# Attention probabilities of a hybrid decoder: two complementary triangles transposed as one tile and parted by 0/1 masks, transposes issued ahead of the value products

## The chip, the core and the metric

The kernel runs on one core of a Trainium2 chip. Its engines are TensorE (PE, matrix products; the profile shows its weight loads as PEld), VectorE (DVE), ScalarE (ACT), GpSimd (POOL, unused here) and SyncE (SP, which issues the DMAs). The metric is device time in microseconds for one call, the median of some runs.

## The reference

Two decoder layers on 256 tokens of width 2048, all in float32. Layer 0 is a recurrent block (RG-LRU) with a SwiGLU FFN, layer 1 a grouped-query attention with a sliding window and attention sinks, with a second FFN. The part that matters here:

```
scores = einsum("bnqhgd,bnkhd->bnhgqk", q, k_band) * (1.0 / sqrt(HEAD_DIM))
mask = window_mask(nblk)            # 0 <= q_pos - k_pos < 128, and the key exists
scores = where(mask, scores, -1e30)
probs = softmax(concatenate([scores, sink], -1), -1)[..., :-1]
out = einsum("bnhgqk,bnkhd->bnqhgd", probs, v_band)
x = x + out.reshape(b, s, N_HEADS * HEAD_DIM) @ w_o
```

There are 32 query heads of 64 features, four K/V heads, and two blocks of 128 tokens. A query of block 0 sees only the keys of its own block that are not after it (a lower triangle). A query of block 1 sees the same triangle of its own block, and of block 0 the keys k > q (in positions inside the block): the complementary triangle.

## The kernel before, in words

Activations are held transposed, features on the partitions and the 256 tokens along the row. Every weight matrix is streamed from HBM as jobs: one job is a tile of 128x1024 (512 KB), loaded by SP four jobs ahead, split three jobs ahead into a high part (ACT, line 259) and a rest (DVE, line 260), and multiplied in 24 matmuls of 256 columns (products, lines 289 to 325; some pairs are merged into one of 512 columns). A group is the run of jobs that fills four PSUM banks: 8 jobs for the q projection w_q (four groups) and for w_o. The first two groups of w_o are interleaved (project, lines 492 to 505): six jobs of the first, six of the second, then the last two of each. Each job of w_o multiplies two of the sixteen attention tiles at[0] to at[15].

All else is background: generators in a list, in order of their start, which stream (line 271) advances twice per job, once in the middle (half_tick) and once at the end (run_bg). A job so has two ticks. run_bg (line 200) keeps an account for DVE and one for ACT. Every helper charges a cost in ns (lines 111 to 137: ACT 100 + 0.833 a column, a DVE tensor_tensor 69 + 1.042 a column, a tensor_scalar 69 + 0.6 a column), at each tick DVE_TICK and ACT_TICK are taken off, but not below -SPARE, and steps run while both accounts are under their tick. In the attention stage these are 740, 900 and 1000 (LATER, line 810). pe (line 115) takes the estimated time of TensorE's extra work off both accounts. A step that yields n rests for n ticks. If a job needs a tile that isn't ready, need (line 213) steps all background tasks, whatever the accounts say, until it is. The program's scheduler may move instructions of one engine past each other where no dependence forbids it; pe_other (line 327) chains the extra TensorE instructions in the order in which they are written.

The attention (attn, line 850) has, for each group of w_q, a q task (line 987): it squares and splits the four q tiles, holds one PSUM bank for three ticks (matmuls with con, a copy, two transposes), and then puts four pairs of heads into todo. One generator, pairs (line 926), works them off, one visit at a time and 19 visits in all (V1 to V19 in what follows). A visit has three parts, each for another pair of heads: values of pair A (values, line 861), transposes of pair B (line 873), scores of a new pair (line 881). Thus the pair that is new in visit n is transposed in visit n+2 and multiplied with the values in visit n+3. After the matmuls, a tick later, the transposes are copied from PSUM by ACT (lines 958 and 959), the value product is split into its two parts (ACT, DVE), which makes at[k] ready, and softmax (line 892) runs for the new pair: per head and query block a masked scaling with its maximum on DVE (line 900), exponentials with sums on ACT, and then four multiplications by the reciprocal of the sum on DVE (lines 918 to 922, through ts, line 131).

A visit needs up to four PSUM banks of the four that MISC allows, so it waits while a q task holds one. It also waits while hold is set, which is from the seventh job of a group to the start of the next group. The next visit comes VISIT = 3 ticks after the last began, or when its softmax is done.

The probabilities of one head are a tile of 128 queries x 384: columns 0 to 127 for block 0 on its own keys, 128 to 255 for block 1 on the keys of block 0, 256 to 383 for block 1 on its own keys. Masked scores become exact zeros. All three parts are transposed, six transposes for two heads.

Of the kernel before, what the change touches and what calls it, by code (L numbers as in the profile page):

```python
# [15 lines left out]
ALU = mybir.AluOpType  # L16

P = 128
D = 2048
T = 256  # L20
# [14 lines left out]

K_ONE, K_BLK, K_SEL0, K_SEL1, K_ID = 0, 128, 256, 384, 512
K_HS, K_MASK = 640, 672
NCON = 672 + 384


class Val:
# [7 lines left out]
class Trunk:  # L49
# [18 lines left out]
    def __init__(self, ctx, tc, dram):  # L68
# [6 lines left out]
        self.par = const.tile([P, NPAR], F32, name="par")  # L75
        self.con = const.tile([P, NCON], F32, name="con")
        self.cc = const.tile([P, 32], F32, name="cc")
# [772 lines left out]
    def attn(self, xs, r, gains, rn):  # L850
        nc, con, par = self.nc, self.con, self.par
# [5 lines left out]
        blocks = ((0, 0, P), (1, P, 3 * P))  # L857
# [3 lines left out]
        def values(k, pT, p):  # L861

            c = (k // 4) * HD
            v0, v1 = (q.ap[:, c:c + HD] for q in self.v)
            o = [p[HD * hh:HD * hh + HD, T:2 * T] for hh in range(2)]
            for hh in range(2):
                self.pe_other(o[hh], v0, pT[0][:, hh * T:(hh + 1) * T], start=True, stop=False)
            for hh in range(2):
                self.pe_other(o[hh][:, P:T], v1, pT[1][:, hh * P:(hh + 1) * P], start=False, stop=True)
            for q in pT:  # L870
                self.free(q)

        def transposes(sc, ps):
            for hh in (1, 0):
                for j in (2, 1, 0):
                    o = ps[0][:, hh * T + j * P:hh * T + j * P + P] if j < 2 else ps[1][:, hh * P:hh * P + P]
                    self.pe_other(o, sc[hh][:, j * P:(j + 1) * P], one, f=nc.tensor.transpose)
            for q in sc:
                self.free(q)

        def scores(k, qs, ps):

            kd = self.kd[k // 4].ap
            for b, c0, c1 in blocks:
                for i, j in ((1, 0), (0, 0), (0, 1)):
                    for hh in range(2):
                        q = slice(HD * hh, HD * hh + HD)
                        self.pe_other(ps[hh][:, c0:c1], qs[q, i * T + b * P:i * T + b * P + P],
                                      kd[q, j * T:j * T + c1 - c0], start=i == 1, stop=j == 1)
            self.free(qs)  # L890

        def softmax(k, rr, ps, sc):
            f = k % 4
            sm = self.half()
            mx, nm, es, den = (sm[:, 4 * i:4 * i + 4] for i in range(4))
            for hh in range(2):
                for b, c0, c1 in blocks:
                    i = b * 2 + hh
                    self.dve += 69 + 1.042 * (c1 - c0)
                    nc.vector.tensor_tensor_reduce(  # L900
                        sc[hh][:, c0:c1], ps[hh][:, c0:c1], con[:, K_MASK + c0:K_MASK + c1],
                        rr[:, b * 8 + f * 2 + hh:b * 8 + f * 2 + hh + 1],
                        par[:, C_SINK + 4 * k + hh:C_SINK + 4 * k + hh + 1], ALU.add, ALU.max,
                        accum_out=mx[:, i:i + 1])
                self.free_mbank(ps[hh])
                yield
            self.ts(nm, mx, -1.0, None, ALU.mult)
            self.tt(es, par[:, C_SINK + 4 * k:C_SINK + 4 * k + 4], mx, ALU.subtract)
            self.a(es, es, AF.Exp)
            for hh in range(2):  # L910
                for b, c0, c1 in blocks:
                    i = b * 2 + hh
                    o = sc[hh][:, c0:c1]
                    self.a(o, o, AF.Exp, bias=nm[:, i:i + 1], accum_out=den[:, i:i + 1])
                yield
            self.tt(den, den, es, ALU.add)
            self.rcp(den, den)
            for hh in range(2):
                for b, c0, c1 in blocks:
                    i = b * 2 + hh  # L920
                    o = sc[hh][:, c0:c1]
                    self.ts(o, o, den[:, i:i + 1], None, ALU.mult)
                yield
            self.free_half(sm)

        def pairs():


            A = B = C = None
            n = 0  # L930
            while n < ND or A or B or C:
                new = None
                if todo and self.kd[todo[0][0] // 4].ready and self.v[0].ready and self.v[1].ready:
                    new = todo.popleft()
                    n += 1
                elif not (A or B or C):
                    yield 1
                    continue
                at_tick = self.tick
                count = 2 * bool(A or B) + 2 * bool(new)  # L940
                while self.hold or self.misc + count > self.MISC or len(self.banks) < count or len(self.slots) < 6:
                    yield 1
                pt = [self.mbank() for _ in range(2)] if A or B else None
                ps = [self.mbank() for _ in range(2)] if new else None
                if A:
                    values(A[0], A[1], pt[1])
                    self.pe(900)
                if B:
                    transposes(B[1], pt)
                    self.pe(700)  # L950
                if new:
                    scores(new[0], new[1], ps)
                    self.pe(900)
                yield 1
                nextA = None
                if B:
                    s = [self.slot(F32) for _ in range(2)]
                    self.a(s[0], pt[0])
                    self.a(s[1][:, 0:T], pt[1][:, 0:T])
                    nextA = (B[0], s)  # L960
                    yield
                if A:
                    s = self.slot()
                    self.split_act(s, pt[1][:, T:2 * T])
                    at[A[0]].ap = s
                    at[A[0]].ready = True
                    yield
                for p in pt or ():
                    self.free_mbank(p)
                A, B, C = nextA, C, None  # L970
                if new:
                    sc = [self.slot(F32) for _ in range(2)]
                    yield from softmax(new[0], new[2], ps, sc)
                    C = (new[0], sc)
                yield max(1, at_tick + self.VISIT - self.tick)
            for q in self.kvs:
                self.free(q)

        for g in range(4):
            def done(ps, g=g):  # L980
# [6 lines left out]
                def task():  # L987
# [41 lines left out]
                    if g == 0:  # L1029
                        self.spawn(pairs())  # L1030
# [50 lines left out]
def constants():  # L1081
    i = np.arange(P)
    con = np.zeros((P, NCON), np.float32)
    con[:, K_ONE:K_ONE + P] = 1.0
    con[:, K_BLK:K_BLK + P] = (i[:, None] // HD) == (i[None, :] // HD)
    con[:, K_SEL0:K_SEL0 + P] = i[:, None] == (i[None, :] % HD)
    con[:, K_SEL1:K_SEL1 + P] = i[:, None] == (HD + i[None, :] % HD)
    con[:, K_ID:K_ID + P] = np.eye(P)
    con[:, K_HS:K_HS + 32] = (i[:, None] // HD) == np.arange(32)[None, :] // 16
    own = np.where(i[None, :] <= i[:, None], 0.0, NEG)  # L1090
    prev = np.where(i[None, :] > i[:, None], 0.0, NEG)
    con[:, K_MASK:K_MASK + 384] = np.concatenate([own, prev, own], axis=1)
    return con


# [35 lines left out]
```

## Time and profile before

| | |
|---|---|
| median of 3 runs | 1989.83 us (1989.81 to 1989.93) |
| span of the profiled execution | 1988.6 us; the page gives no time of that execution outside the span |
| scores of the first visit | at 1072.85 us of the span |
| values of the last visit | at 1208.33 us |
| matmuls that are not of a weight stream, L334 | 1.6% of the chain that ended last |
| granted TensorE clock | full in all 40 slices |

Times inside the trace are us from the start of the span. A row of the timeline gives start, length, engine, line, operation, out<-in by the program's names (buffer numbers left out), shape and count; a bracket at its end is idle time of the engine before it, and what ended it. For a matmul the shape 128*64 128x256 is a stationary operand of 128 rows and 64 columns, and 256 columns streamed. b is any PSUM bank, s any slot of SBUF, con the table of constants. So b<-con,s is a transpose of probabilities, b<-s,s with 128*64 is a value product and with 64*128 a score, b<-s,hi and b<-s,lo are the weight streams, and b<-s,con and b<-con,h belong to a q task. The first instruction of such a chain may stand under line 331 and the others under 334. A row of a group has busy time, mean ns of one, and idle time before. In a row of windows stand the window, its length, and the busy time and count of PE, PEld, DVE, ACT, POOL, the clock, the DMA share and GB/s.

### The profile page before, as it was taken

Reading aid. Unit: us, or ns where it says so; the run is one execution under the profiler, and the core shown is the slowest. Engines: PE = TensorE matmul, PEld = TensorE weight load, DVE = VectorE, ACT = ScalarE, POOL = GpSimd, SP = SyncE. Lnnn points to the kernel's source line nnn. Section 1 sums busy time; section 2 is a strip of 40 time slices with the busy share of each in tenths; the row PEclk is TensorE's granted clock in tenths of the full one; section 3 lists DMA queues with packets and bytes.
Section 4 is the critical chain, followed back from the end, with each engine's and each line's share of the span. In section 5 each row is a group of like instructions: output and inputs, shape, how many; then the busy total and the mean of one; then the engine's idle time right before and its main releaser. Section 6 shows DMA issues by size and latency. Waiting matters only on the chain.

```text
span 1988.6 us, 40066 instructions
## 1 busy us (share of the span) xinstructions
PE 1982.0 (100%) x16684; PEld 1935.5 (97%) x16684; DVE 1271.2 (64%) x2049; ACT 1067.9 (54%) x1624; POOL 0.2 (0%) x4
## 2 busy tenths in 40 slices
PE   9999999999999999999999999999999999999999
PEld 9999999999999999999999889999999999999999
DVE  8988876556556655545668786755565565554453
ACT  7798655444444444444556775544454454444442
POOL 0000000000000000000000000000000000000000
PEclk9999999999999999999999999999999999999999
DMA  8555655565556555556555435565566656656663
GB/s 279 185 187 182 211 191 192 196 196 191 192 195 196 191 192 196 195 191 194 197 186 167 134 101 163 188 197 195 191 193 196 195 191 194 197 193 203 204 208 128
DMA packets 105302, 376.58 MB, mean 189 GB/s; under 512 B 11808, under 2 KB 14240, under 8 KB 105120
## 3 DMA queue, kind: packets, MB, share of 16 engines
q1 hardware_dynamic: 104832, 373.88, 57.8%
q8 instruction: 130, 2.13, 0.4%
q14 instruction: 52, 0.43, 0.1%
q10 hardware_dynamic: 288, 0.14, 0.0%
HBM read 371.88 MB, written 2.10 MB: 188 GB/s over the span
## 4 chain that ended last, share of the span: by engine, by line
PE 99%; ACT 0%; DVE 0%; DMA 0%; issue 0%; ACTq 0%
PE b L323 94%; PE b L334 2%; PE b L641 1%; PE b L331 1%; PE b L832 1%; ACT s L113 0%; PE b L321 0%; PE b L841 0%; PE b L842 0%; PE b L843 0%; DMA x<-in_x 0%; DVE s L131 0%; DVE lo L260 0%; ACT L113 0%; DVE s L122 0%
## 5 line engine op out<-in xcount | busy, mean ns | idle before, releaser
L323 PE MATMUL b<-s,hi 128*128 128x256 f32 (+1 forms) x10276 | 1431.9, 285 | 0.4 <-ACT s L113 0.4
L323 PEld LDWEIGHTS b<-s,hi 128*128 128x128 f32 x10276 | 1313.4, 188 | 30.4 <-ACT s L113 0.7
L260 DVE TENSOR_TENSOR lo<-raw,hi 128x1024 fp32r<-128x1024 f32 (+1 forms) x705 | 861.4, 1223 | 651.2 <-ACT hi L259 648.1
L259 ACT ACTIVATE hi<-raw 128x1024 fp32r<-128x1024 f32 (+1 forms) x705 | 745.7, 1059 | 817.7 <-PE b L323 756.7
L323 PE MATMUL b<-s,lo 128*128 128x256 f32 x5504 | 831.8, 277 | 0.0
L323 PEld LDWEIGHTS b<-s,lo 128*128 128x128 f32 x5504 | 720.4, 188 | 2.4 <-issue 0.8
L113 ACT ACTIVATE s<-h 128x256 fp32r<-128x256 f32 (+1 forms) x106 | 40.8, 411 | 23.8 <-DVE h L122 23.8
L113 ACT ACTIVATE t<-b 128x256 f32<-128x256 f32 x136 | 49.8, 374 | 2.5 <-PE b L323 0.3
L113 ACT ACTIVATE s<-x,par 128x256 fp32r<-128x256 f32 x80 | 38.6, 499 | 19.3 <-DVE x L122 13.6
L113 ACT ACTIVATE s<-s 128x256 f32<-128x256 f32 (+1 forms) x112 | 39.6, 409 | 5.7 <-DVE s L126 5.5
L113 ACT ACTIVATE h<-h 128x256 f32<-128x256 f32 (+1 forms) x104 | 38.8, 375 | 2.1
L113 ACT ACT_TABLE_LOAD x30 | 38.5, 1283 | 0.5
L126 DVE SCALAR_TENSOR_TENSOR s<-x,par,s 128x256 fp32r<-128x256 f32 x80 | 37.5, 482 | 1.4 <-ACT s L113 0.8
L122 DVE TENSOR_TENSOR h<-b,rstd 128x256 f32<-128x256 f32 x100 | 37.6, 417 | 0.0
L122 DVE TENSOR_TENSOR x<-x,b 128x256 f32<-128x256 f32 x64 | 24.1, 418 | 21.0 <-PE b L323 21.0
L113 ACT ACTIVATE s<-s,h 128x128 f32<-128x128 f32 x64 | 28.3, 443 | 13.3 <-DVE h L131 13.2
L122 DVE TENSOR_TENSOR h<-h,rstd 128x256 f32<-128x256 f32 x94 | 35.4, 419 | 0.0
L122 DVE TENSOR_TENSOR h<-h,h 128x256 f32<-128x256 f32 x88 | 35.0, 420 | 0.4 <-ACT h L113 0.4
L122 DVE TENSOR_TENSOR s<-h,s 128x256 fp32r<-128x256 f32 x88 | 35.2, 420 | 0.1
L122 DVE TENSOR_TENSOR h<-b,t 128x256 f32<-128x256 f32 x92 | 34.6, 417 | 0.0
L122 DVE TENSOR_TENSOR s<-s,s 128x256 fp32r<-128x256 f32 (+1 forms) x80 | 30.9, 422 | 3.5 <-ACT s L113 3.5
L334 PE MATMUL b<-s,s 64*128 64x256 f32 (+3 forms) x292 | 29.0, 302 | 0.1
(99 smaller groups left out, 566.4 us busy)
## 6 DMA issues: line engine op xcount, KB each, us to landing
raw<-in_ffn_in SPq DMA_DIRECT2D x352, 512.0 KB, 3.5
raw<-in_ffn_out SPq DMA_DIRECT2D x176, 512.0 KB, 4.3
raw<-in_lru_in SPq DMA_DIRECT2D x63, 512.0 KB, 3.6
raw<-in_lru_out SPq DMA_DIRECT2D x32, 512.0 KB, 3.7
raw<-in_w_q SPq DMA_DIRECT2D x32, 512.0 KB, 3.3
raw<-in_w_o SPq DMA_DIRECT2D x32, 512.0 KB, 3.3
raw<-in_gate SPq DMA_DIRECT2D x8, 512.0 KB, 3.9
raw<-in_kv SPq DMA_DIRECT2D x8, 512.0 KB, 4.3
```

Of the source, the lines that this page charges most:

```text
L113: self.nc.scalar.activation(out, in_, func, **kw)
L122: self.nc.vector.tensor_tensor(out, a, b, op)
L126: self.nc.vector.scalar_tensor_tensor(out, a, s, b, op0, op1)
L259: self.nc.scalar.activation(hi[:, q], raw[:, q], AF.Copy)
L260: self.nc.vector.tensor_tensor(lo[:, q], raw[:, q], hi[:, q].bitcast(F32), ALU.subtract)
L323: self.nc.tensor.matmul(*args, **kw)
L331: self.other = self.ins(f(*args, **kw))
L334: self.other = self.ins(f(*args, **kw))
L641: nc.tensor.matmul(out[j], (hi if high else lo)[:, c:c + P], x2[kt][:, q:q + T], start=kt == 0 and high > q, stop=kt == 1 and not high)
L832: nc.tensor.matmul(ps[f][:, 0:T], w0, x2[kt][:, q:q + T], start=k0 + kt == 0 and high > q, stop=k0 + kt == ND - 1 and not high)
```

## The change

The two parts of block 1 never overlap: where one is a probability the other is an exact zero. After the change softmax adds them in place (one tensor_tensor of 128 columns a head), so the multiplications by the reciprocals have 128 columns each. The sum is transposed once, four transposes for two heads where there were six. When the transposes are taken from PSUM, ACT copies block 0 of both heads (256 columns in one strided copy), and DVE multiplies block 1 twice by a 0/1 triangle from con, once for the keys of block 0 and once for those of block 1. con grows by those two triangles, 256 columns. In a visit the transposes are issued ahead of the values, and the estimates given to pe change from 900 and 700 to 450 and 800.

```diff
-NCON = 672 + 384
+K_PREV, K_OWN = 672 + 384, 672 + 512
+NCON = 672 + 640
...
         def transposes(sc, ps):
             for hh in (1, 0):
-                for j in (2, 1, 0):
-                    o = ps[0][:, hh * T + j * P:hh * T + j * P + P] if j < 2 else ps[1][:, hh * P:hh * P + P]
+                for j in (1, 0):
+                    o = ps[0][:, hh * T + j * P:hh * T + j * P + P]
...
             for hh in range(2):
-                for b, c0, c1 in blocks:
+                o = sc[hh][:, P:2 * P]
+                self.tt(o, o, sc[hh][:, 2 * P:3 * P], ALU.add)
+                for b in range(2):
                     i = b * 2 + hh
-                    o = sc[hh][:, c0:c1]
+                    o = sc[hh][:, b * P:b * P + P]
                     self.ts(o, o, den[:, i:i + 1], None, ALU.mult)
...
+                if B:
+                    transposes(B[1], pt)
+                    self.pe(450)
                 if A:
                     values(A[0], A[1], pt[1])
-                    self.pe(900)
-                if B:
-                    transposes(B[1], pt)
-                    self.pe(700)
+                    self.pe(800)
...
                     s = [self.slot(F32) for _ in range(2)]
-                    self.a(s[0], pt[0])
-                    self.a(s[1][:, 0:T], pt[1][:, 0:T])
+                    pair = lambda q: q.rearrange("p (h b q) -> p h b q", h=2, b=2)
+                    src, dst = pair(pt[0][:, :]), pair(s[0][:, :])
+                    last = s[1][:, 0:T].rearrange("p (h q) -> p h q", h=2)
+                    self.a(dst[:, :, 0, :], src[:, :, 0, :])
+                    for o, c in ((dst[:, :, 1, :], K_PREV), (last, K_OWN)):
+                        self.tt(o, src[:, :, 1, :], con[:, c:c + P].unsqueeze(1).broadcast_to([P, 2, P]), ALU.mult)
...
+    con[:, K_PREV:K_PREV + P] = prev.T == 0
+    con[:, K_OWN:K_OWN + P] = own.T == 0
```

## Prediction

> **What bounds the kernel now.** I read the page first: the shares of busy time, then the chain that ended last.
>
> ```profile
> PE 1982.0 (100%) x16684; PEld 1935.5 (97%) x16684; DVE 1271.2 (64%) x2049; ACT 1067.9 (54%) x1624; POOL 0.2 (0%) x4
> PE 99%; ACT 0%; DVE 0%; DMA 0%; issue 0%; ACTq 0%
> ```
>
> TensorE sets the time, so a saved TensorE instruction is worth its slot in the queue, and VectorE (DVE) has a third of the span free. But these are averages, and the change lives in one stage of 136 us. So next the windows over that stage (columns: window, length, PE, PEld, DVE, ACT busy).
>
> ```profile
> 1137.00:1149.00 12.00, 12.00 (x100) 10.87 (x100) 7.98 (x26) 8.79 (x28) 0.00 (x0) 1.00 0.40 132
> 1149.00:1160.00 11.00, 11.00 (x100) 9.53 (x99) 8.37 (x27) 8.60 (x26) 0.00 (x0) 1.00 0.44 144
> 1160.00:1168.00 8.00, 8.00 (x79) 6.63 (x78) 7.79 (x31) 6.82 (x14) 0.00 (x0) 1.00 0.46 134
> 1168.00:1178.00 10.00, 8.61 (x82) 7.03 (x81) 8.09 (x37) 8.36 (x32) 0.00 (x0) 1.00 0.15 55
> 1178.00:1184.00 6.00, 5.62 (x57) 4.15 (x57) 5.93 (x25) 4.83 (x16) 0.00 (x0) 1.00 0.28 87
> ```
>
> From 1160 to 1184 DVE is busy 21.8 of 24.0 us, and TensorE is not full. Now the timeline of TensorE: all transpose blocks from the fourth visit on (a visit is one turn of the loop in pairs; V1 is the first), with the first block, V3, ahead of them.
>
> ```profile
> 1088.23 0.27 PE L331 MATMUL b<-con,s 128*128 128x128 f32 x1
> 1088.33 0.71 PE L334 MATMUL b<-con,s 128*128 128x128 f32 x5
> 1088.97 0.96 PE L334 MATMUL b<-s,s 64*128 64x128 f32 x12
> ...
> 1100.20 0.88 PE L334 MATMUL b<-con,s 128*128 128x128 f32 x6
> 1107.07 0.88 PE L334 MATMUL b<-con,s 128*128 128x128 f32 x6
> 1119.50 0.87 PE L334 MATMUL b<-con,s 128*128 128x128 f32 x6
> 1131.56 0.87 PE L334 MATMUL b<-con,s 128*128 128x128 f32 x6
> 1138.41 0.88 PE L334 MATMUL b<-con,s 128*128 128x128 f32 x6
> 1150.72 0.88 PE L334 MATMUL b<-con,s 128*128 128x128 f32 x6
> 1161.57 0.88 PE L334 MATMUL b<-con,s 128*128 128x128 f32 x6
> 1164.06 0.88 PE L334 MATMUL b<-con,s 128*128 128x128 f32 x6
> 1170.68 0.87 PE L334 MATMUL b<-con,s 128*128 128x128 f32 x6 [1.04 <-DVE s L131]
> 1173.67 0.88 PE L334 MATMUL b<-con,s 128*128 128x128 f32 x6 [0.29 <-DVE s L131]
> 1179.64 0.87 PE L334 MATMUL b<-con,s 128*128 128x128 f32 x6 [0.38 <-DVE s L131]
> 1182.16 0.88 PE L334 MATMUL b<-con,s 128*128 128x128 f32 x6
> 1190.50 0.88 PE L334 MATMUL b<-con,s 128*128 128x128 f32 x6
> ```
>
> Two regimes. Up to V9 (1150.72) visits come three to a group of the q projection, with the long gaps (1107 to 1119, 1138 to 1150) where hold is set. V10 to V15 come in pairs, two visits back to back and then one job: here w_o already wants values that don't exist, need() drives the loop, and TensorE waits for DVE's normalisation (L131) three times, 1.7 us in all. That is the place where DVE is the bound.
>
> **The change, part by part.** First TensorE. One full visit, values, transposes, scores, next main matmul:
>
> ```profile
> 1118.70 0.43 PE L331 MATMUL b<-s,s 128*64 128x256 f32 x1
> 1120.30 0.95 PE L334 MATMUL b<-s,s 64*128 64x128 f32 x12
> 1121.19 0.50 PE L321 MATMUL b<-s,hi 128*128 128x512 f32 x1
> ```
>
> Values 0.80 (1118.70 to 1119.50), six transposes 0.80, scores 0.89: 2.49 us. Behind a main block the six take 0.74 (1088.23 to 1088.97), their first two starting 0.10 apart, nearer 0.11 over the block. With four of them in front: 0.74 - 2 x 0.11 = 0.52, then 0.80 and 0.89: 2.21, so 0.28 saved in each of 13 full visits (V4 to V16), and 0.22 in V3, V17 and V18: 13 x 0.28 + 3 x 0.22 = 4.3 us. Values followed directly by scores are not in the trace; the switch costs between nothing and the 0.06 by which transposes after values exceed those after main, so the sum lies between 4.3 and 5.1; I keep 4.3. The Trainium skill ("TensorE: Matmul & The Clock Gate", Part 4) gives about 275 ns for a transpose inside a kernel; counted so, the 32 removed ones would be worth 8.8 us and the sum below some 5 us lower, but the six starts within 0.74 us speak against counting durations.
>
> ScalarE loses a 512-wide copy and turns two copies into one of 256; its time is off the path, and nothing is gained where DVE is late.
>
> DVE gains two adds of 128, two mask products of 256 read from PSUM, and narrows two multiplies. Prices:
>
> ```profile
> L122 DVE TENSOR_TENSOR h<-b,t 128x256 f32<-128x256 f32 x92 | 34.6, 417 | 0.0
> L900 DVE CUSTOM_DVE_ANT_0 s<-b,con,par 128x256 f32<-128x256 f32 x32 | 17.3, 541 | 0.0
> L131 DVE TENSOR_SCALAR s<-s,h 128x256 f32<-128x256 f32 x32 | 11.2, 349 | 0.0
> L131 DVE TENSOR_SCALAR s<-s,h 128x128 f32<-128x128 f32 x32 | 9.1, 284 | 0.5
> L122 DVE TENSOR_TENSOR rr<-rr 128x16 f32<-128x16 f32 x12 | 2.1, 175 | 0.4
> 1117.89 1.08 DVE L122 TENSOR_TENSOR s<-b,t 128x256 f32<-128x256 f32 x3
> ```
>
> Three 256-wide products in a row take 1.08, 0.36 each in the queue. Between 175 ns at 16 columns and 417 at 256 the slope is 1.0 ns a column, so a 128-wide add costs 0.36 - 0.13 = 0.23, taken as 0.22. Per visit: 2 x 0.22 + 2 x 0.36 - 2 x 0.065 = 1.03 us. Ends: adds from 0.17 (the row of 16) to 0.42, products from 0.36 to 0.54 (the L900 row, which reads PSUM and con too): 0.93 to 1.79. The skill ("VectorE: DVE Perf Modes", Mode 2x_2P) says that an fp32 multiply by a scalar makes two results a cycle and an fp32 product of two tensors one; by that the fold pays full rate to save half rate, which the rows bear out (65 ns saved, 0.22 us paid), and the sum stays.
>
> Larger than the price is what the program's own accounts do with it, since they place the visits. In this stage a tick allows 740 for DVE, credit is cut to -1000 at each tick, and a job has two ticks. Before, a visit charges in its next tick 336 (split) + 538 + 538 + 145 from -1000, which is 557: it stops only on ScalarE's account. The tick after brings it to 729, under 740, so it ends, and V5 follows V4 by VISIT = 3 ticks. After: two products 671, split 336, 538, 538 give 1083 and stop it; next tick 343 + 145 + 176 + 494 = 1158, stop; next 418 + 494 = 912, stop; then it ends, and the next visit is at 5 ticks at the earliest. A group has 16 ticks, of which hold closes the last four. Before, in group 3: V3 at tick 0, V4 at 6 (when the q task returns its bank), V5 at 9. After: the q task comes a tick later behind V3, V4 is at 7, and 7 + 5 = 12 is closed. In group 4, V5 at 0 delays the q task by two ticks, V6 at 8, and 13 is closed. So **two visits slip**: by the third w_o job V7 is done where V9 was, and four pairs are forced (V8 to V15) and not three.
>
> The stretch, then, by rows (1160.77 is the first value matmul of V10):
>
> ```profile
> 1155.44 0.40 PE L331 MATMUL b<-s,con 128*32 128x256 f32 x1
> 1157.48 1.52 PE L323 MATMUL b<-s,hi 128*128 128x256 f32 x12
> 1158.99 0.33 PE L331 MATMUL b<-con,h 128*128 128x128 f32 x1
> 1160.77 0.43 PE L331 MATMUL b<-s,s 128*64 128x256 f32 x1
> 1183.85 2.15 PE L323 MATMUL b<-s,hi 128*128 128x256 f32 x16
> ```
>
> Before: V10 at 1160.77, transposes of V12 9.91 later, of V14 8.96 later, of V15 2.52 later, the main job 1.69 after that, at 1183.85. After: the third w_o job would begin at 1157.48 less two full visits (4.98), less what was saved until then (0.22 + 4 x 0.28 = 1.34), less the q task's two steps that now fall behind it (0.76): 1150.4. There need() first runs those steps, two matmul groups with a copy between, about 1.5 us (0.57 + 0.19 of TensorE, a copy of some 0.4, waits). Then the intervals grow by DVE's new work, as DVE is full: 9.91 + two visits' products 1.44 + one net fold 0.31 = 11.66; twice 8.96 + 2.06 = 11.02; 2.52 + 0.8 (most of one visit's 1.03) = 3.3; and 0.52 + 0.80 + 0.89 = 2.2 for V15. Sum 40.7, so main at 1191.1, 7.3 later than before. V16 to V18 give back 0.28 + 0.44 = 0.7. Net +6.6: **1996.4 us**, counting from the median 1989.8, which stands 1.2 over the profiled span of 1988.6; that rest is untouched. In this stretch the TensorE saving buys nothing, and the order costs: values used to run while DVE finished, now they stand behind the wait.
>
> The larger con is 0.13 MB more of one early DMA; TensorE waits nowhere for a DMA in the table of waits, so 0, at most 0.5 us.
>
> **The rivals.** (1) Slack takes it all: visits keep their places and DVE's gaps (7.98 of 12.00 busy at 1137) hold the 16 x 1.03 us; only TensorE's 4.3 is left, 1985.5, faster. It needs a DVE that is under its limit from 1160 to 1184, and the rows show 5.93 of 6.00 at the end. It turns to a loss where DVE's new work in the forced stretch exceeds its idle 2.2 us there, which is two visits' worth. (2) No slip, but DVE binds in the same three pairs: V10 at 1158.9, then 11.66, 11.02, 3.3, 2.2 give 1187.0, +3.2 - 0.7: 1992.3. It holds if the emission in the queue falls out better than the accounts say. (3) The stretch is worse: products at their upper end (0.76 more a visit, six visits) and scores half a microsecond later behind values in four pairs, so the chain scores, exponentials, normalisation is late as well: 6.6 us more, 2003.0. For it: ScalarE is also at 8.36 of 10.00 there. Against: it loses its wide copies.
>
> **How the numbers follow.** Forecast 1996.4 with 0.58 (its own range 1994 to 2000); rival 1 0.08, rival 2 0.17, rival 3 0.17. About 0.2%, 4 us, is what a measurement of this kernel can tell from no change: below 1985.9 is faster, above 1993.8 slower. Rival 1 is faster, 0.08; rival 2 the same, 0.17; forecast and rival 3 slower, 0.75. The range leaves out rival 1 and the upper part of rival 3: 1989.0 to 2003.0.
>
> **What would show it.** Right: 64 transposes, none idle before 1150; two visits a group; four forced pairs; waits of transposes on DVE of 8 us or more in all; DVE full for some 35 us before the last forced job. Wrong: three visits a group still, or waits that stay near 1.7 us, or main matmuls waiting for lo instead.

## The result, and the profile after

The kernel after takes 1993.97 us (median of 9 runs, 1993.44 to 1998.32), the kernel before in the same comparison 1989.93 (9 runs, 1989.62 to 1991.37): a ratio of 1.0022, interval 1.0014 to 1.0030. It is slower by 4.0 us, 0.2%. The profiled execution of after took 1993.44 us, with a span of 1991.7. In the rows below, a line of after is one higher than the same line of before (L334 is now L335).

First the page of after, engines and chain, to be held against those of before:

```profile
PE 1976.4 (99%) x16658; PEld 1930.0 (97%) x16658; DVE 1284.9 (65%) x2113; ACT 1062.6 (53%) x1608; POOL 0.2 (0%) x4
PE 97%; DVE 2%; ACT 1%; DMA 0%; issue 0%; SPq 0%; DVEq 0%; ACTq 0%
```

TensorE did 5.6 us less work (1982.0 to 1976.4), and yet the span is 3.1 longer: its idle time went from 6.6 to 15.3 us. The chain that ended last now runs through VectorE and ScalarE for 3% of the span, where it was 0%. Two instants of the timeline say where. The first scores of V1 and the first matmul of the norm that follows w_o, before:

```profile
1072.85 0.33 PE L331 MATMUL b<-s,s 64*128 64x128 f32 x1
...
1279.33 0.59 PE L331 MATMUL b<-acc,con 128*128 128x256 f32 x2
```

and after:

```profile
1071.90 0.33 PE L332 MATMUL b<-s,s 64*128 64x128 f32 x1
...
1282.42 0.59 PE L332 MATMUL b<-acc,con 128*128 128x256 f32 x2
```

From the one to the other 206.48 us before, 210.52 after: 4.04 more, about what the medians differ by (that the two agree to the hundredth is chance). After is 0.95 early at V1, so its whole span is only 3.1 longer. Those 0.95 us arise ahead of the attention, where the two programs do the same work, and have to be added when instants of the two traces are compared. Next the waits of TensorE after (total us, times, longest):

```profile
PE b L332 <- DVE s L132: 3.3, 3, 1.3
PE b L324 <- ACT s L114: 3.1, 3, 1.1
PE b L335 <- ACT h L114: 1.9, 1, 1.9
PE b L269 <- DVE lo L266: 1.2, 1, 1.2
PE b L324 <- DVE s L123: 0.9, 1, 0.9
PE b L324 <- ACT hi L260: 0.6, 1, 0.6
PE b L335 <- DVE s L132: 0.5, 1, 0.5
PE b L324 <- DVE h L901: 0.4, 1, 0.4
```

Transposes wait 3.8 us for the normalisation (L132), where it was 1.7. The weight matmuls (L324) wait 5.0 us for what ScalarE and VectorE have not yet written or freed, where it was 0.4, and the q task waits 1.9 for its copy. The wait at L269 is the same 1.2 us before. The timeline of TensorE through the forced stretch, from the q task's step that opens it:

```profile
1148.69 0.40 PE L332 MATMUL b<-s,con 128*32 128x256 f32 x1
...
1151.23 0.44 PE L335 MATMUL b<-con,h 128*128 128x128 f32 x2 [1.90 <-ACT h L114]
1151.51 0.60 PE L335 MATMUL b<-con,s 128*128 128x128 f32 x4
...
1153.72 0.66 PE L335 MATMUL b<-con,s 128*128 128x128 f32 x4
...
1161.49 0.30 PE L332 MATMUL b<-con,s 128*128 128x128 f32 x1 [1.27 <-DVE s L132]
...
1166.53 2.16 PE L324 MATMUL b<-s,hi 128*128 128x256 f32 x16
1168.52 1.10 PE L324 MATMUL b<-s,lo 128*128 128x256 f32 x8
1170.79 0.30 PE L332 MATMUL b<-con,s 128*128 128x128 f32 x1 [1.16 <-DVE s L132]
...
1181.15 0.30 PE L332 MATMUL b<-con,s 128*128 128x128 f32 x1 [0.90 <-DVE s L132]
...
1183.39 1.50 PE L324 MATMUL b<-s,hi 128*128 128x256 f32 x8
1185.31 1.21 PE L324 MATMUL b<-s,hi 128*128 128x256 f32 x8 [0.42 <-DVE h L901]
1186.36 0.63 PE L324 MATMUL b<-s,lo 128*128 128x256 f32 x4
1186.83 0.28 PE L324 MATMUL b<-s,hi 128*128 128x256 f32 x1
1186.95 0.60 PE L335 MATMUL b<-con,s 128*128 128x128 f32 x4
...
1190.13 1.51 PE L324 MATMUL b<-s,hi 128*128 128x256 f32 x10 [0.90 <-ACT s L114]
```

The transposes at 1151.51 are those of V8, then V9, V10 (1161.49), V12 (1170.79), V14 (1181.15) and V15 (1186.95): four forced pairs, and the first is V8. Between V14 and V15 stand 8 + 8 + 4 + 1 = 21 weight matmuls; before, V15 followed V14 with none between. Last the windows over this stretch (window, length, then PE, PEld, DVE, ACT busy):

```profile
1149.00:1160.00 11.00, 8.23 (x82) 6.46 (x74) 9.60 (x46) 8.95 (x27) 0.00 (x0) 1.00 0.33 97
1160.00:1170.00 10.00, 7.88 (x74) 6.21 (x73) 9.87 (x48) 6.65 (x24) 0.00 (x0) 1.00 0.17 54
1170.00:1180.00 10.00, 8.04 (x72) 6.36 (x72) 8.83 (x40) 5.91 (x23) 0.00 (x0) 1.00 0.17 53
1180.00:1192.00 12.00, 9.77 (x87) 7.88 (x86) 10.19 (x46) 6.00 (x24) 0.00 (x0) 1.00 0.16 46
```

TensorE is idle for 9.1 of these 43 us (33.92 busy), more than its idle time grew in the whole span. VectorE is busy 38.49 of 43: heavy, but not full.

### The profile page after: what moved, and what is told of

Same layout as the page of the kernel before. It is cut to its first block, busy times and chain, and to the rows that moved or that the text cites. A ratio compares the mean times of both kernels' runs of the same rounds, so it can differ in the third digit from the quotient of the medians.

```text
span 1991.7 us, 40053 instructions
## 1 busy us (share of the span) xinstructions
PE 1976.4 (99%) x16658; PEld 1930.0 (97%) x16658; DVE 1284.9 (65%) x2113; ACT 1062.6 (53%) x1608; POOL 0.2 (0%) x4
## 4 chain that ended last, share of the span: by engine, by line
PE 97%; DVE 2%; ACT 1%; DMA 0%; issue 0%; SPq 0%; DVEq 0%; ACTq 0%
PE b L324 93%; PE b L642 1%; PE b L335 1%; PE b L833 1%; DVE s L901 1%; ACT s L114 0%; DVE s L123 0%; PE b L332 0%; DMA raw<-in_lru_in 0%; DVE lo L261 0%; PE b L322 0%; DVE s L132 0%; PE b L842 0%; PE b L843 0%; PE b L844 0%
## 5 line engine op out<-in xcount | busy, mean ns | idle before, releaser
L324 PE MATMUL b<-s,hi 128*128 128x256 f32 (+1 forms) x10282 | 1431.7, 284 | 5.2 <-ACT s L114 3.1
L324 PEld LDWEIGHTS b<-s,hi 128*128 128x128 f32 x10282 | 1312.3, 188 | 36.9 <-ACT s L114 3.7
L324 PE MATMUL b<-s,lo 128*128 128x256 f32 x5504 | 830.2, 276 | 0.0
L324 PEld LDWEIGHTS b<-s,lo 128*128 128x128 f32 x5504 | 719.5, 188 | 1.6
L335 PE MATMUL b<-s,s 64*128 64x256 f32 (+3 forms) x318 | 28.3, 310 | 0.0
```

The lines of the kernel that those rows point to most:

```text
L324: self.nc.tensor.matmul(*args, **kw)
L335: self.other = self.ins(f(*args, **kw))
```

## The experiments

The theory was that the slip of two visits, which the program's accounts make, is the loss, and that VectorE's new work costs something beside it in the forced pairs. The rivals: that VectorE's work alone costs it, whatever the places of the visits; and that the new order costs it. The kernel before took 1990.35, 1990.13 and 1990.11 us in the three sets of runs that follow.

**The accounts of before.** The kernel after, every instruction kept, but charged as the kernel before was.

```diff
+                self.dve += 76.8 - 202.376
...
+                    self.act += 526.496
...
+                    self.dve -= 2 * 335.752
...
-                    self.pe(450)
+                    self.pe(700)
...
-                    self.pe(800)
+                    self.pe(900)
```

> The changed kernel, its work untouched, but charged to the accounts what the old visit was charged (and 700 and 900 credited), so that the visits fall on the old ticks: three to a group, V9 ahead of the third w_o job. Theory (the accounts let two visits slip, and DVE's new work binds in the forced stretch): three forced pairs again, the slip's share of the loss is gone, the rest stays: 1991 to 1992.5. Rival A (DVE's work alone is the loss, wherever the visits stand): as the changed kernel, 1994. Rival B (TensorE's saving is all that counts once the ticks are right): 1985.

Measured: 1989.63 us (1989.14 to 1990.66), ratio 0.9998 (0.9989 to 1.0006). The same instructions, begun at other ticks, are 4.3 us cheaper than the kernel after, and no slower than the kernel before. The slip is the loss. The time came out 1.4 us under the expectation, so VectorE's work costs less than I thought. There are three forced pairs, V10 to V15, of which V12 to V15 wait for VectorE:

```profile
1168.12 0.30 PE L332 MATMUL b<-con,s 128*128 128x128 f32 x1 [1.27 <-DVE s L132]
1171.37 0.63 PE L335 MATMUL b<-con,s 128*128 128x128 f32 x4 [0.94 <-DVE s L132]
1178.19 0.30 PE L332 MATMUL b<-con,s 128*128 128x128 f32 x1 [1.22 <-DVE h L123]
1181.75 0.66 PE L335 MATMUL b<-con,s 128*128 128x128 f32 x4 [0.54 <-DVE s L132]
```

The waits of the transposes add up to 4.0 us here, no less than after, where it was 3.8. What fell is the rest: with the forced pair V8 and V9 went the 1.9 us behind the q task's copy, and the weight matmuls wait 2.7 us and not 5.0. Together that is 4.2 us, and TensorE's idle time is 4.1 lower (15.3 to 11.2).

**The slip alone.** The kernel before, every instruction kept, but charged as the kernel after is.

```diff
+                self.dve += 202.376 - 76.8
...
-                    self.pe(900)
+                    self.pe(800)
...
-                    self.pe(700)
+                    self.pe(450)
...
+                    self.act -= 526.496
+                    self.dve += 2 * 335.752
```

> The kernel before, with all its own instructions, but charged to the program's accounts as the kernel after is charged (each visit 671 more for VectorE from the products, 202 less 77 more for each add, 526 less for ScalarE, pe 450 and 800). So the visits begin at the ticks of the kernel after: V4 and V5 slip, four pairs are forced. Theory (the slip alone is the loss, whatever VectorE has to do): 1992.5 to 1995. Rival (the slip costs only because VectorE's new work is met once more in each forced pair): 1990 to 1991, not to be told from the kernel before.

Measured: 1998.55 us (1997.84 to 1998.96), ratio 1.0042 (1.0029 to 1.0054). The slip needs none of the new work to cost time. But 8.4 us are more than I expected, and the windows show why (window, length, PE, PEld, DVE, ACT, POOL busy, granted clock):

```profile
1150.17:1153.58 3.41, 1.47 (x16) 0.85 (x14) 1.38 (x7) 2.73 (x10) 0.00 (x0) 1.00 0.45 156
1153.58:1163.82 10.24, 9.26 (x52) 6.56 (x54) 5.03 (x23) 4.43 (x11) 0.00 (x0) 0.50 0.14 51
```

Behind a stretch in which TensorE was busy for less than half the time, the granted clock stood at a half for 10.24 us. At most 5.1 us are lost to it, so the slip itself costs at least 3.3. On the pages of the two kernels TensorE's busy time grew by 3.5 us (1982.0 to 1985.5) and its idle time by 5.0 (6.6 to 11.6). Between 3.3 and 5.0 is, but for a tenth at its upper end, inside the expectation. In the profiled run of the kernel after the clock stayed full, and its slip cost 4.3.

**The products taken off VectorE**, at the ticks of after. The two products become copies on ScalarE; the parting by masks is left out.

```diff
-                    for o, c in ((dst[:, :, 1, :], K_PREV), (last, K_OWN)):
-                        self.tt(o, src[:, :, 1, :], con[:, c:c + P].unsqueeze(1).broadcast_to([P, 2, P]), ALU.mult)
+                    for o in (dst[:, :, 1, :], last):
+                        self.nc.scalar.activation(o, src[:, :, 1, :], AF.Copy)
+                        self.dve += 335.752
```

> The changed kernel with its accounts and ticks kept, but the two DVE products with the triangles replaced by two copies on ScalarE; the masking is left out. Theory: four forced pairs stay, but DVE has 0.72 us less in each of the some seven visits that it binds: 4 to 5 us less than the changed kernel, 1989 to 1990. Rival A (the slip alone is the loss): 1994. Rival B (ScalarE's copies were what paid before): slower than 1994.

Measured: 1996.1 us (1994.05 to 1998.63), ratio 1.0028 (1.0017 to 1.0039): a miss of the theory; by its number rival B came in. With the visits in their late places a lighter VectorE bought nothing. Part of it is the clock again: here it stood at a half in two windows of 3.41 us, from 1151.06 and from 1181.78, each behind one in which TensorE was busy for half the time or less (1.65 and 1.44 us). The second of them:

```profile
1178.37:1181.78 3.41, 1.44 (x14) 1.03 (x11) 2.57 (x14) 1.64 (x8) 0.00 (x0) 1.00 0.00 0
1181.78:1185.19 3.41, 3.41 (x18) 3.00 (x19) 1.56 (x9) 3.12 (x10) 0.00 (x0) 0.50 0.02 5
```

Twice 1.7 us, at most, are 3.4, which would put the profiled run (1994.9) at 1991.5, still above what I expected. Whether it was ScalarE's copies that cost the rest, as rival B has it, stays open. The run therefore settles nothing on the products; the next ones, at the ticks of before, do.

**TensorE's part alone, and the adds alone**, both at the ticks of before. The first has four transposes, the new order, no adds, and copies on ScalarE for the products; the sum in block 1 and the parting are left out. Both edits below are its own. The second has the lower one alone: it keeps the adds and leaves out the parting. Both are charged as before by lines like those of the first experiment, which are left out here.

```diff
-                self.tt(o, o, sc[hh][:, 2 * P:3 * P], ALU.add)
+                self.dve += 76.8
...
-                        self.tt(o, src[:, :, 1, :], con[:, c:c + P].unsqueeze(1).broadcast_to([P, 2, P]), ALU.mult)
+                        self.nc.scalar.activation(o, src[:, :, 1, :], AF.Copy)
```

> Four transposes and the new order, old accounts and ticks, no add and no product with a triangle (block 1 of the probabilities and its masking are left out); the copies stay on ScalarE. So only TensorE's part of the change is left. Theory: the saving of 4.3 to 5.6 us is real where TensorE binds, and lost only in the three forced pairs: 1985 to 1986.5. Rival (a removed transpose is worth its 275 ns of duration): 1981. Rival (TensorE's saving goes into waits): 1989.9.

> The kernel after with the accounts of before, its adds kept, its two mask products on VectorE replaced by copies on ScalarE (block 1 isn't parted by the masks: that part of the computation is left out). Between the kernel without adds and products (1986.92) and the one with both (1989.63). Theory (VectorE's busy time counts, so the 2.7 us between them go by duration: two net adds 0.31, products 0.72 a visit): 1987.4 to 1988.2. Rival (the adds stand in the chain from the exponentials to the transposes and the products don't, so the adds cost most of it): 1988.8 to 1989.6.

Measured: 1986.92 us without adds and products (1986.14 to 1987.72, ratio 0.9983, 0.9974 to 0.9992), 1988.16 with the adds (1987.8 to 1990.77, ratio 0.9992, 0.9983 to 1.0001). With both it was 1989.63. The steps add up: TensorE's part gains 3.4, the adds cost 1.2, the products 1.5, the slip 4.3; together +3.6. Measured is +4.0, and the missing 0.4 is the kernel before, which took 1990.35 in the set of runs that the 3.4 is counted from and 1989.93 in the first comparison. The first expectation, 1985 to 1986.5, is missed by 0.4. For the adds it was 1987.4 to 1988.2 by VectorE's busy time; it holds. The runs with the adds alone and with both overlap, so how the 2.7 us part into 1.2 and 1.5 is loose; those without and with both don't, so the 2.7 stand. They are the price over copies on ScalarE, which is busier by these (1061.1 to 1069.3 us). VectorE's groups of after in the attention stage give the size of the work behind them (busy us, mean ns, idle before):

```profile
L123 DVE TENSOR_TENSOR s<-b,con 128x256 f32<-128x256 f32 x32 | 12.4, 417 | 1.3 <-ACT s L114 1.1
L123 DVE TENSOR_TENSOR s<-s 128x128 f32<-128x128 f32 x32 | 9.2, 288 | 5.6 <-ACT s L114 5.4
```

A product takes 417 ns, as the row of 256 columns that the prediction priced it by, and an add 288, where the prediction's slope between 175 and 417 gives 288 for 128 columns. Adds and products make VectorE 13.4 us busier (1269.5 to 1282.9 on the pages of the two kernels), and 2.7 of that reached the end, a fifth.

**The order.** Transposes ahead of values in the kernel before, and values ahead of transposes in the kernel after with the accounts of before.

```diff
+                if B:
+                    transposes(B[1], pt)
+                    self.pe(700)
                 if A:
                     values(A[0], A[1], pt[1])
                     self.pe(900)
-                if B:
-                    transposes(B[1], pt)
-                    self.pe(700)
```

> The kernel before with one edit: transposes ahead of values, six transposes, old work, same ticks. Theory: in the forced pairs the values no longer run while DVE ends the normalisation, up to 0.8 us for each of three or four waits, less about 0.06 to 0.1 us for one switch fewer in each of 15 visits: 1989.5 to 1992. Rival (the order is free): 1989.9. Rival (the order is the saving): 1988.5.

> The kernel after with the accounts of before (1989.63), and the values issued ahead of the transposes again. Theory (as the prediction has it, values ran while VectorE finished, and now stand behind the wait; 0.8 us of work in each of the four waits): 1988.0 to 1989.2. Rival (the order is worth nothing, since the program's scheduler fills the waits with weight matmuls, and the transposes behind the main matmuls are 0.06 cheaper in 13 visits): 1989.6 to 1990.6.

Measured: 1991.25 us for the new order in before (1990.6 to 1993.22, ratio 1.0005, 0.9996 to 1.0014), 1990.73 for the old order in the other (1989.75 to 1993.05, ratio 1.0004, 0.9995 to 1.0012, where the new order gave 0.9998). Each order looks 0.9 to 1.1 us the better in the kernel that it belongs to, but the first interval holds 1, and the intervals of the other two overlap. The first time is inside its theory's range; the second missed its theory and lies 0.1 above the rival's. That the order costs anything in time, as the prediction said, is not shown. The mechanism that it named does show in the waits of the new order with the old work:

```profile
PE b L331 <- DVE s L131: 2.3, 2, 1.6
PE b L334 <- DVE s L131: 1.2, 2, 1.0
```

The transposes wait 3.5 us there, 1.7 in the kernel before. In the kernel with TensorE's part alone, which has no new work on VectorE, it is 3.1. With the order put back in the other kernel it falls from 4.0 to 0.5, and blocks of values wait 1.7 in their place. So the transposes wait longer by the order, more than by the new work, and most of the rise from 1.7 to 3.8 in the kernel after should come with it.

**Two ways to unload VectorE.** In the first, block 0 is normalised by ScalarE; in the second, ScalarE copies all columns and GpSimd multiplies in SBUF. Both with the accounts of before.

```diff
-                    self.ts(o, o, den[:, i:i + 1], None, ALU.mult)
+                    if b:
+                        self.ts(o, o, den[:, i:i + 1], None, ALU.mult)
+                    else:
+                        nc.scalar.activation(o, o, AF.Copy, scale=den[:, i:i + 1])
+                        self.dve += 145.8
...
-                        self.tt(o, src[:, :, 1, :], con[:, c:c + P].unsqueeze(1).broadcast_to([P, 2, P]), ALU.mult)
+                    self.nc.scalar.activation(dst[:, :, :, :], src[:, :, :, :], AF.Copy)
...
+                        self.nc.gpsimd.tensor_tensor(o, dst[:, :, 1, :], con[:, c:c + P].unsqueeze(1).broadcast_to([P, 2, P]), ALU.mult)
```

> The kernel after with the accounts of before (1989.63 when it ran), and of the four multiplications by the reciprocals in a visit the two of block 0 on ScalarE: VectorE 0.44 us lighter a visit, ScalarE some 0.8 heavier. Theory (with the ticks right, VectorE's new work in the three forced pairs is what is left of the loss, 2.7 us for 1.03 a visit): 1988 to 1989.2, faster than the kernel before. Rival (ScalarE, 6.65 of 10 us busy in the forced stretch of the kernel after, is as late as VectorE): 1989.6 to 1992.

> The kernel after with the accounts of before (1989.63), its two mask products a visit moved from VectorE to GpSimd, which stands idle: ScalarE copies all 512 columns from PSUM, GpSimd multiplies in SBUF. VectorE 0.7 us lighter a visit. Theory (VectorE's work in the three forced pairs is the 2.7 us between the kernel with and the one without its new work, and the products are 1.5 of them): 1988.0 to 1988.8. Rival (GpSimd's products, whose duration no trace of this kernel shows, are so late that the next values wait for them in the forced pairs): 1990 to 1994.

Measured: 1990.33 us with ScalarE (1989.86 to 1991.04, ratio 1.0001, 0.9992 to 1.0010), 1991.92 with GpSimd (1991.33 to 1994.47, ratio 1.0013, 1.0004 to 1.0022). Both theories missed, both rivals hold. In the first, transposes now wait for ScalarE's multiplications (L929):

```profile
PE b L335 <- ACT s L929: 1.4, 2, 0.9
```

In the second, GpSimd's group and the wait that it makes:

```profile
L968 POOL TENSOR_TENSOR s<-s,con 128x256 f32<-128x256 f32 x32 | 27.2, 852 | 1179.4 <-ACT s L966 1178.1
```

```profile
PE b L335 <- POOL s L968: 1.1, 1, 1.1
```

A product takes 852 ns there and 417 on VectorE, and one block of values waits 1.1 us for it. That is about half of the 2.3 us by which this kernel stands above 1989.63; the rest is not traced.

**No forced pair at all.** More credit and closer visits, in the kernel after, in the kernel before, and in the one with TensorE's part alone (with the same parts of the computation left out).

```diff
-    VISIT = 3
+    VISIT = 2
...
-    LATER = (740.0, 900.0, 1000.0)
+    LATER = (740.0, 900.0, 2000.0)
```

> The kernel after with its own accounts, but with LATER = (740, 900, 2000) and VISIT = 2 in place of (740, 900, 1000) and 3: more credit carried over the ticks, and a visit as soon as two ticks after the last. By the accounts 16 visits are then begun when the third job of w_o starts, not 7, and no pair is forced. Theory (the loss is made in the forced pairs alone; outside them VectorE's new work lies in its gaps and TensorE's saving counts): 1983 to 1987, and 3 to 4.5 below the kernel before with the same two settings. Rival (visits packed closer make TensorE wait for the rest parts that VectorE splits off the weights): 1988 or more.

> The kernel before with LATER = (740, 900, 2000) and VISIT = 2, as the control to the kernel after with the same settings. No pair is forced by the accounts. Theory (the 5 us that TensorE idles between 1166 and 1184 are most of its 6.6 us of idle time, and go with the forced pairs): 1986 to 1988.5. Rival (the idle time moves to the splits of the weights): 1989.5 to 1991.

> Four transposes, new order, no adds, the products replaced by copies on ScalarE (the parting by masks, and in block 1 the sum, are left out), accounts charged as before, and LATER = (740, 900, 2000), VISIT = 2. What TensorE's saving is worth with no forced pair and nothing for VectorE to pay. Theory (without forced pairs VectorE's new work is free): within 1 us of the kernel after with the same settings. Rival (VectorE's 1.03 us a visit costs outside the forced pairs too): 2 to 3 us below it.

Measured: 1993.0 us for after (1992.59 to 1995.57, ratio 1.0016, 1.0008 to 1.0025), 1989.91 for before (1989.29 to 1990.29, ratio 0.9998, 0.9989 to 1.0007), 1987.11 for TensorE's part (1986.35 to 1987.46, ratio 0.9985, 0.9976 to 0.9993). This was meant to be the better version, and it is none: all three theories missed. By the number the rivals of the first two hold, and the third kernel is further below after than its rival said. The expectation for before rested on a figure that I had misread: TensorE idles 1.39 us from 1168 to 1178 and 0.38 from 1178 to 1184, so 1.8 us in the forced pairs and not 5. There was little to win.

More telling is the first: without any forced pair, after is 5.9 us above TensorE's part alone, where with three forced pairs it was 2.7 (the ticks of the two differ somewhat, since after is charged for its new work). So the theory that VectorE's work costs only in forced pairs falls. The waits of the transposes of after, in these settings:

```profile
PE b L332 <- DVE h L123: 4.2, 4, 1.1
PE b L332 <- DVE s L132: 2.1, 2, 1.1
```

These are 6.3 us; in the kernel with TensorE's part alone they wait 1.9. The timeline of after around V3 (VectorE, then TensorE):

```profile
1078.92 0.28 DVE L123 TENSOR_TENSOR s<-s 128x128 f32<-128x128 f32 x1
...
1079.21 0.52 DVE L901 CUSTOM_DVE_ANT_0 s<-b,con,par 128x256 f32<-128x256 f32 x1
...
1079.65 0.87 DVE L132 TENSOR_SCALAR s<-s,h 128x128 f32<-128x128 f32 x4
...
1080.67 0.30 PE L332 MATMUL b<-con,s 128*128 128x128 f32 x1 [1.04 <-DVE h L123]
```

V3 transposes what V1 scored. With visits so close, VectorE has put the masked scaling of V2 (L901) between V1's sum and V1's four multiplications, which end 0.15 us before the transposes start; TensorE waits 1.04. Four of the waits are of this kind, 1.04 to 1.07 us each. Transposes that follow the normalisation this closely pay for it, forced or not. I take from it that the distance counts; no run here varies it alone.

## Why the prediction was right, and where it was not

**The direction and the mechanism were right.** I forecast 1996.4 from a slip of two visits, and 1993.97 came, just under the 1994 to 2000 of the forecast itself, inside the whole range, and slower than before by just over the bound of 1993.8. That the accounts make the slip, and the slip the loss, is shown from both sides: the new work at the old ticks, TensorE's saving set against it, costs nothing (1989.63); the old work at the new ticks costs 8.4 us, of which at most 5.1 are the clock's.

**TensorE's saving** was sized at 4.3, up to 5.1, V17 and V18 counted in, though my list of all transpose blocks ends with V16 (theirs stand at 1197.44 and 1203.28). TensorE's busy time fell by 5.6, and with the other costs away 3.4 us reached the end; the transposes of that kernel wait 1.4 us longer than before (3.1 to 1.7). In the forced stretch a full visit takes what I priced, 2.21: V8's transposes begin at 1151.51, V9's at 1153.72.

**The price of VectorE's new work** was right for the single instruction and too high in sum. VectorE's busy time rose by 11.7 us at the ticks of before (1271.2 to 1282.9) and by 13.7 at its own (1284.9): 0.73 to 0.86 a visit, where I had 1.03 and a lower end of 0.93. Rival 1 (slack takes it all, 1985.5) is out, though most of it is hidden: 2.7 us of 13.4 reach the end.

**The places of the visits** came as worked out: V8 opens the stretch, and four pairs are forced.

**The stretch is the step that failed: "Then the intervals grow by DVE's new work, as DVE is full".** Its sum looks right: the weight job behind V15 was to come at 1191.1, and it came at 1190.13, or 1191.1 with the 0.95 added. That is luck, since the parts were not these and their errors cancel:

| | predicted | measured |
|---|---|---|
| third w_o job to V8's transposes | 1.5 | 2.82 |
| V8 to V10 | 11.66 | 9.98 |
| V10 to V12 | 11.02 | 9.30 |
| V12 to V14 | 11.02 | 10.36 |
| V14 to V15 | 3.3 | 5.80 |
| V15 to the weight matmuls | 2.2 | 3.18 |
| sum | 40.7 | 41.44 |

Three intervals came out 4.1 us shorter than I priced. The kernel before had 9.91, 8.96 and 8.96 us there, so they grew by 0.1, 0.3 and 1.4, and I had counted 1.75, 2.06 and 2.06. The error is in "as DVE is full". Before, V12 to V14:

```profile
1170.68:1179.64 8.96, 8.22 (x77) 6.65 (x77) 7.98 (x36) 7.30 (x24) 0.00 (x0) 1.00 0.17 61
```

After, V10 to V12:

```profile
1161.49:1170.79 9.30, 7.66 (x73) 6.21 (x73) 9.21 (x42) 5.16 (x18) 0.00 (x0) 1.00 0.19 58
```

VectorE did 1.23 us more (7.98 to 9.21), 0.89 of it in time that it had been idle before, and only 0.34 lengthened the interval. V12 to V14 grew more, with VectorE busy for 9.19 of 10.36 us and a wait of 1.06 for ScalarE inside (at 1174.16). V14 to V15 grew by 2.5 more than priced, but not in idle time: 21 weight matmuls stand there. At 0.124 us each (16 from 1166.53 to 1168.52) they are 2.6 us of work that the kernel before did only after V15. So at the same weight matmul the delay was not 7.3 but 1191.08 - 1183.85 - 2.6 = 4.6 us; less the 0.6 that V16 to V18 give back, it is the 4.04 between the two instants above. With the sum right by luck, the forecast's excess of 2.4 us is that term: I counted instants of a job's start, and not the work done by then.

Rival 3's longer stretch (2003.0) did not come, since the intervals were shorter than priced and not longer. The same oversize shows in rival 2. Its world, no slip and three pairs, is the kernel with the accounts of before: priced at 1992.3, it took 1989.63, 2.7 less. V12 to V14, priced at 11.02, took 10.07 there (1168.12 to 1178.19).

**What I missed in the stretch** is on both sides. Of the 2.8 us that the q task's two steps took (1148.69 to 1151.51), 1.9 were a wait for ScalarE's copy. And the transposes waited 3.8 us for VectorE, not the 8 that I named as the sign. Beside them weight matmuls waited 5.0 us, 3.7 for ScalarE and 1.3 for VectorE, which I had not priced.

**Open.** The order's worth is below what the runs resolve. By the instants, TensorE was 0.8 us further at the third job than my savings give (1148.69 plus 0.95 against 1150.4). I had also taken off both steps of the q task (0.76), though the second stands behind that job before as well (1158.99), so the right sum gives 1150.6 and the gap is 0.95. It lies in the weight matmuls: counted on TensorE from start to start, those between one and the same weight matmul ahead of V3 (1082.77 before, 1081.83 after) and the third w_o job took 56.1 us before and 55.2 after. Why the same work took less is open.

## What to carry to other kernels

Where a planner places work by estimates, a change acts twice: by its instructions, and by what it is charged. Run it once with the old charges, and the old kernel once with the new ones, before blaming the instructions. And compare two traces at the same piece of work, not at the same named event: a scheduler that fills waits with later work makes an interval longer without losing it.

## What was not expected of the hardware

The granted TensorE clock fell to a half without a long gap. In the slipped kernel of before the clock fell at 1153.58, inside this gap, when TensorE had been idle for 1.93 us:

```profile
1154.08 0.69 PE L334 MATMUL b<-con,h 128*128 128x128 f32 x2 [2.43 <-ACT h L113]
```

The stretches at half clock lasted 3.41 us (twice) and 10.24, which is three times 3.41. The windows of 3.41 us ahead of them had TensorE busy for 1.65, 1.44 and 1.47 us. A window of the kernel after with 1.73 busy was followed by full clock (its place is counted in steps of 3.41 us from where the clock rose at the start of that trace):

```profile
1147.60:1151.01 3.41, 1.73 (x18) 1.12 (x17) 2.81 (x8) 3.12 (x11) 0.00 (x0) 1.00 0.33 83
1151.01:1154.42 3.41, 3.19 (x32) 2.40 (x34) 2.57 (x13) 2.33 (x6) 0.00 (x0) 1.00 0.74 227
```

The Trainium skill ("TensorE: Matmul & The Clock Gate", Part 1) gives an activity window of 3413 ns, and the 3.41 and 10.24 agree. The Trainium skill ties the fall to an idle window, with gaps over about 3.4 us as its rule, and has a kernel whose short idle times between groups of matmuls did it too. Here no gap in the windows ahead of the falls was longer than 1.93 us, and a window that was about half busy was enough. Where exactly the limit lies these runs don't tell: with the order put back a window with 1.94 us busy (1168.84 to 1172.25) was followed by half clock, while the 1.73 of the kernel after was not. The falls stand in forced stretches, among waits, which so have a second price: one run of the kernel after, at 1998.32 us, had a mean clock of 0.996, and the four of its runs at 1993.44 to 1993.85 had 1.0.

On GpSimd the Trainium skill ("GPSIMD Engine Reference", Section 3.1) has an elementwise fp32 sum of two tensors, 2048 elements long, at 1.96 times VectorE's time. The products here, of 256 columns, give 852 to 417 ns, 2.04 times; VectorE's read PSUM and GpSimd's SBUF.
